# A gated hybrid encoder block on one core: a new order of its work groups, planned with other durations

## The chip, the cores and the metric

The kernel runs on one core of a Trainium2 chip. The metric is device time in microseconds (us) of one execution. Engines are named as in the profile: PE multiplies matrices (PEld loads its weights), DVE and POOL do elementwise work, ACT does activations and copies, SP issues nearly all the DMAs.

## The reference, cut to what matters

One layer over x (1024 rows, width 1024), in float32:

```
h = rmsnorm(x);  q, k, v, z_a, u_b, v_b, z_b, g_a, g_b = split(h @ w_in)
y_a = stick_breaking_attention(q, k, v) * silu(z_a)       # 8 heads of 64
y_b = spatial_gating(gelu(u_b), gelu(v_b)) * silu(z_b)    # 8 groups of 64, chunks of 128 rows
merged = sigmoid(g_a) * (y_a @ w_up_a) + sigmoid(g_b) * (y_b @ w_up_b)
out = rmsnorm(x + merged @ w_out)
```

In stick-breaking attention the weight of key s for query t is sigmoid(z[t,s]) times the product of sigmoid(-z) over the keys between s and t, so every row of scores needs a running product (a scan) over its keys. Spatial gating normalises gelu(v_b) per group, mixes it along 128 rows with a masked weight, adds a bias and multiplies by gelu(u_b).

## The kernel before, in words

**Numbers.** Every product is made of three float32r products (high·high, high·low, low·high). `hi_lo` (L214) makes the parts: ACT casts the high part, DVE (or POOL) subtracts to get the low part.

**Projections.** `project` (L528) makes one pair of 128-wide column tiles of h @ w_in for all 1024 rows by seven block products of 12 matmuls (84 matmuls of 512 columns), with sums and differences of weight blocks on POOL and DVE before them and sums of results after them. It uses the PSUM tiles X, Y, Z, four raw weight tiles `a` (7 slots) loaded by SP, split weights `b` (8 slots) and `f2`. There are 20 such work groups, each with a `use` of its four results:

- `make_kq` (4): split and store keys and queries to DRAM for one pair of heads.
- `make_za` (2): SiLU of attention's gate path. `make_gates` (8): sigmoid of the merge gates, ACT and a store only.
- `make_u`, `make_zb`, `make_vb` (2 halves of each): the spatial gate. `make_vb` is the long one: a GELU, transposes, reductions, scalings, a mixing product and transposes back, through the tiles `r`, `ak`, `e`, `tr`, `o`, `z`.

**Attention.** `head(p, h)` (L820) loads keys, queries and values (7 loads into 4 `k` tiles) and goes over two chunks of 512 queries. `attn_row` (L650) makes scores (PE, tile `z`), two sigmoids (ACT, tiles `ak`, `r`), the scan (DVE: `scan`, L198, on diagonal blocks; `scan_mult`, L191, on the others) and the product of the two (DVE on diagonal blocks, POOL on the others). `attn_step` (L674) transposes the weights (tile `tr`), splits them (`e`) and multiplies with the values (`o`). Heads share `r`, `ak`, `e`, `tr`, `o`, `z` with `make_vb`; `project` uses none of these.

**After the heads.** `up_b`, `up_a` (products of y_b, y_a with the up weights), then the output product and the last norm.

**What sets the order.** Nothing is issued as it is written. Each operation becomes a `Task` with an engine and a cost (L104 to L231). `Plan.issue` (L234) then plays the program against these costs: an engine that is free takes the ready task of the lowest priority number, a result reaches another engine `LAT` later, a tile is given out in the order in which the code first named the tiles of its tag. The order so found, engine by engine and for SP's DMA queue, is written into the program. On the chip each engine runs its own list in that order and waits where an operand is late; costs change the lists, never an operation.

For PE the priority number is the place in the code: what was written first goes first whenever it is ready, and later groups fill in. For the others it is that place plus an offset: -9000 for `project`'s own steps, -6000 for the `use` of a group called by `ahead` (L813), 0 otherwise. L827 to L854 name the groups in the order kq0 u0 zb0 vb0 za0 h0 u1 zb1 vb1 h1 kq1 g0 g1 h2 kq2 g2 h3 za1 g3 h4 kq3 g4 h5 g5 h6 g6 h7 g7 (h for heads, g for merge gates); those from u1 on that aren't heads go through `ahead`.

Of the kernel before, what the change touches and what calls it, by code (L numbers as in the profile page):

```python
# [10 lines left out]
F32 = mybir.dt.float32  # L11
# [9 lines left out]
EPS = 1e-6  # L21
GELU_C = 0.044715
GELU_S = 1.5957691216057308
LAT = 0.7
SCAN = 2.0


# [56 lines left out]


class Task:
    __slots__ = ("eng", "cost", "fn", "bufs", "deps", "users", "idx", "prio", "tail", "waiting", "ready", "end")


class Plan:  # L90
# [13 lines left out]
    def add(self, eng, cost, fn, out, ins, tail=0.0):  # L104
        t = Task()
        t.eng, t.cost, t.fn, t.tail = eng, cost, fn, tail
        t.idx = len(self.tasks)
        t.prio = t.idx + (self.offset if eng != "PE" else 0)
        t.deps, t.users, t.bufs = set(), [], []
        for v, write in [(v, True) for v in out] + [(v, False) for v in ins]:  # L110
            b = v.buf
            for box, w, other in b.touched:
                if (w or write) and other is not t and all(a < d and c < e for (a, e), (c, d) in zip(box, v.box)):
                    t.deps.add(other)
            b.touched.append((v.box, write, t))
            if b.order is None:
                b.order = self.tag_count.get(b.tag, 0)
                self.tag_count[b.tag] = b.order + 1
            if b not in t.bufs:
                t.bufs.append(b)  # L120
                b.left += 1
        for o in t.deps:
            o.users.append(t)
        self.tasks.append(t)


    def mm(self, out, lhsT, rhs, start, stop, **kw):
        self.add("PE", max(0.109, rhs.n * 0.000417 + 0.0135),
                 lambda: self.nc.tensor.matmul(out.ap(), lhsT=lhsT.ap(), rhs=rhs.ap(), start=start, stop=stop, **kw),  # L129
                 [out], [lhsT, rhs])  # L130

# [30 lines left out]

    def tt(self, out, in0, in1, op, eng="DVE"):
        e = self.nc.vector if eng == "DVE" else self.nc.gpsimd
        near = in0.buf.psum or in1.buf.psum
        cost = out.n * (0.001042 if near else 0.00135) + 0.15 if eng == "DVE" else out.n * 0.00252 + 0.24
        self.add(eng, cost, lambda: e.tensor_tensor(out=out.ap(), in0=in0.ap(), in1=in1.ap(), op=op),  # L167
                 [out], [in0, in1])

# [17 lines left out]
                 [out], [in_])  # L187

    def scan_mult(self, out, in_, init=None):
        self.add("DVE", in_.n * 0.00255 + 0.14,  # L190
                 lambda: self.nc.vector.tensor_tensor_scan(out.ap(), in_.ap(), in_.ap(),  # L191
                                                           1.0 if init is None else init.ap(), op0=ALU.mult,
                                                           op1=ALU.bypass),
                 [out], [in_] + ([] if init is None else [init]))

    def scan(self, out, in_, floor, init):
        self.add("DVE", in_.n * 0.00255 + 0.14,
                 lambda: self.nc.vector.tensor_tensor_scan(out.ap(), in_.ap(), floor.ap(), init, op0=ALU.mult,  # L198
                                                           op1=ALU.max), [out], [in_, floor])

# [31 lines left out]


    def issue(self):  # L234
        now, seq = 0.0, 0
        events = []
        ready = {}
        busy = {}
        turn = {}
        free = dict(self.slots)  # L240
        order = []
        for t in self.tasks:
            t.waiting, t.ready = len(t.deps), 0.0
            busy.setdefault(t.eng, 0.0)
            ready.setdefault(t.eng, [])
            if not t.deps:
                heapq.heappush(ready[t.eng], (t.prio, t.idx, t))

        def can_start(t):
            need = {}  # L250
            for b in t.bufs:
                if not b.held:
                    need.setdefault(b.tag, []).append(b.order)
            for tag, orders in need.items():
                nxt = turn.get(tag, 0)
                if free[tag] < len(orders) or sorted(orders) != list(range(nxt, nxt + len(orders))):
                    return False
            return True

        done = 0  # L260
        while done < len(self.tasks):
            started = False
            for eng, heap in ready.items():
                if busy[eng] > now + 1e-9:
                    continue
                skipped = []
                pick = None
                while heap:
                    item = heapq.heappop(heap)
                    if can_start(item[2]):  # L270
                        pick = item[2]
                        break
                    skipped.append(item)
                for item in skipped:
                    heapq.heappush(heap, item)
                if pick is None:
                    continue
                for b in pick.bufs:
                    if not b.held:
                        b.held = True  # L280
                        free[b.tag] -= 1
                        turn[b.tag] = turn.get(b.tag, 0) + 1
                order.append(pick)
                pick.end = now + pick.cost
                busy[eng] = pick.end
                seq += 1
                heapq.heappush(events, (pick.end, seq, 0, pick))
                done += 1
                started = True
            if started:  # L290
                continue
            if not events:
                stuck = [(t.idx, t.eng, [(b.tag, b.order, b.held, turn.get(b.tag, 0), free[b.tag]) for b in t.bufs])
                         for h in ready.values() for _, _, t in sorted(h)[:4]]
                raise RuntimeError(f"no operation can start: {stuck[:12]}")
            now = events[0][0]
            while events and events[0][0] <= now + 1e-9:
                _, _, kind, t = heapq.heappop(events)
                if kind == 1:
                    heapq.heappush(ready[t.eng], (t.prio, t.idx, t))  # L300
                elif kind == 2:
                    free[t] += 1
                elif kind == 0:
                    for u in t.users:
                        lag = t.tail if t.eng == "DMA" else 0.0 if u.eng == t.eng else LAT
                        u.ready = max(u.ready, now + lag)
                        u.waiting -= 1
                        if u.waiting == 0:
                            seq += 1
                            heapq.heappush(events, (max(u.ready, now), seq, 1, u))  # L310
                    for b in t.bufs:
                        b.left -= 1
                        if b.left == 0 and b.tag in free:
                            seq += 1
                            heapq.heappush(events, (now + t.tail + LAT, seq, 2, b.tag))
        self.length = max(t.end for t in self.tasks)
        for t in order:
            ins = t.fn()
            if t.eng != "DMA":
                self.tc.keep_in_program_order(ins)  # L320
# [9 lines left out]
def hybrid_block(  # L330
# [270 lines left out]
    def make_kq(p):  # L601
        def use(j, half, v, in_psum):
            hi, lo = buf("f2", dt=F32R), buf("f2", dt=F32R)
            pl.hi_lo(hi.all, lo.all, v, near(in_psum))
            pl.store(kq_hi[p][j, :, half_of(half)], hi.all)
            pl.store(kq_lo[p][j, :, half_of(half)], lo.all)
        project(KQ + p, use)

    za = [buf("d", (P, S)) for _ in range(4)]
# [203 lines left out]
    def ahead(fn, *args):  # L813
        pl.offset = -6000
        fn(*args)
        pl.offset = 0
# [7 lines left out]
                sums_of[p, ch] = buf("os")  # L824
            attn_step(*parts, p, h, ch, sums_of[p, ch])

    make_kq(0)  # L827
    make_u(0)
    make_zb(0)
    make_vb(0)  # L830
    make_za(0)
    head(0, 0)
    ahead(make_u, 1)
    ahead(make_zb, 1)
    ahead(make_vb, 1)
    head(0, 1)
    ahead(make_kq, 1)
    ahead(make_gates, 0)
    ahead(make_gates, 1)
    head(1, 0)  # L840
    ahead(make_kq, 2)
    ahead(make_gates, 2)
    head(1, 1)
    ahead(make_za, 1)
    ahead(make_gates, 3)
    head(2, 0)
    ahead(make_kq, 3)
    ahead(make_gates, 4)
    head(2, 1)
    ahead(make_gates, 5)  # L850
    head(3, 0)
    ahead(make_gates, 6)
    head(3, 1)
    ahead(make_gates, 7)  # L854


    ys = {}
# [192 lines left out]
```

## Time and profile before

| | us |
|---|---|
| median of 3 runs (lowest, highest) | 766.57 (766.36, 766.86) |
| the profiled execution, its own time | 766.53 |
| span of the trace in it | 764.7 |

The span runs from the first to the last instruction, 1.8 us less than the execution's time. The stretches of the program in this trace, by the tiles that PE writes: loads, norm and values to 70 us; groups kq0 to za0 and u1 from 70 to 198; head 0 with zb1 and vb1 from 198 to 250; kq1 and g0 until head 1 begins at 306; seven heads with the other ten groups and `up_b` until 632; then `up_a`, the output product and the last norm. A busy time counts a matmul from its start to its modelled end, and matmuls overlap, so short gaps between them don't show.

### The profile page before, as it was taken

How to read it: one execution, taken by the hardware profiler on the slowest of the kernel's cores; microseconds unless marked ns; L12 is line 12 of the kernel's file. 1: busy time of each engine (PE TensorE's matmuls, PEld its weight loads, DVE VectorE, ACT ScalarE, POOL GpSimd, SP SyncE). 2: the span in 40 equal slices, each digit the busy share in tenths (PEclk: the TensorE clock that was granted, in tenths of full speed). 3: DMA queues.
4: the chain of work that ended last, by engine and by line, in shares of the span. 5: the costliest groups of instructions: out<-in, count | busy, mean ns of one | idle time of the engine just before them, and what ended most of it. 6: DMA issues, size and time to landing. Idle time of an engine off the chain costs nothing.

```text
span 764.7 us, 10791 instructions
## 1 busy us (share of the span) xinstructions
PE 735.0 (96%) x3524; PEld 606.4 (79%) x3524; DVE 575.0 (75%) x788; ACT 433.5 (57%) x920; POOL 308.8 (40%) x298
## 2 busy tenths in 40 slices
PE   4989999999889999999999999999999999999996
PEld 3877788888777888887888888878888887888885
DVE  4868754688899787898999988897998878841122
ACT  6636474756756755666757676676867433411122
POOL 1500637497666576274345538234140300013110
PEclk9999999999999999999999999999999999999999
DMA  9412494424344375454543656354597677760022
GB/s 338 176 64 96 144 255 159 146 96 138 113 127 127 103 212 185 141 166 137 153 124 114 191 165 180 108 137 127 173 311 255 213 237 231 252 228 1 29 82 111
DMA packets 69177, 121.31 MB, mean 159 GB/s; under 512 B 7296, under 2 KB 17024, under 8 KB 69120
## 3 DMA queue, kind: packets, MB, share of 16 engines
q1 hardware_dynamic: 67968, 118.52, 49.3%
q10 hardware_dynamic: 1152, 2.10, 0.7%
q8 instruction: 28, 0.46, 0.3%
q14 instruction: 29, 0.24, 0.1%
HBM read 81.27 MB, written 39.32 MB: 158 GB/s over the span
## 4 chain that ended last, share of the span: by engine, by line
PE 83%; DVE 9%; issue 3%; DMA 2%; ACT 2%; POOL 1%; SPq 0%; POOLq 0%; DVEq 0%; ACTq 0%
PE Y L129 22%; PE X L129 21%; PE Z L129 18%; PE z L129 9%; PE o L129 8%; PE tr L133 5%; DVE b L167 2%; DVE ak L198 1%; DVE ak L191 1%; DMA k<-in_x_dram 1%; DVE e L167 1%; DMA k<-d 1%; DVE T L167 1%; DVE f L167 1%; DVE r L167 1%
## 5 line engine op out<-in xcount | busy, mean ns | idle before, releaser
L129 PE MATMUL Y<-T,b 128*128 128x512 f32 x672 | 180.0, 398 | 1.6 <-ACT b L157 1.3
L129 PE MATMUL X<-T,b 128*128 128x512 f32 x660 | 177.9, 398 | 0.0
L129 PE MATMUL Z<-T,b 128*128 128x512 f32 x540 | 145.2, 397 | 0.0
L129 PEld LDWEIGHTS Y<-T,b 128*128 128x128 f32 x672 | 122.3, 188 | 26.0 <-ACT b L157 1.7
L157 ACT CAST b<-a 128x512 fp32r<-128x512 f32 (+1 forms) x152 | 93.6, 617 | 81.9 <-PE Y L129 22.5
L129 PEld LDWEIGHTS X<-T,b 128*128 128x128 f32 x660 | 119.8, 188 | 22.8 <-POOL b L167 0.4
L167 DVE TENSOR_TENSOR b<-a,b 128x512 fp32r<-128x512 f32 (+1 forms) x112 | 99.4, 889 | 28.8 <-ACT b L157 20.0
L129 PEld LDWEIGHTS Z<-T,b 128*128 128x128 f32 x540 | 98.1, 188 | 18.3
L167 POOL TENSOR_TENSOR b<-a,b 128x512 fp32r<-128x512 f32 x40 | 60.7, 1516 | 119.8 <-ACT b L157 106.6
L198 DVE TENSOR_TENSOR_SCAN ak<-ak,c 128x128 f32<-128x128 f32 (+1 forms) x64 | 72.8, 1141 | 3.5 <-ACT ak L146 3.4
L167 POOL TENSOR_TENSOR a<-a,a 128x512 f32<-128x512 f32 x40 | 61.5, 1537 | 28.9 <-DVE b L167 15.3
L167 POOL TENSOR_TENSOR f<-f,f 128x512 f32<-128x512 f32 (+1 forms) x38 | 56.2, 1484 | 36.0 <-ACT f L146 14.7
L157 ACT CAST e<-tr 128x512 fp32r<-128x512 f32 (+1 forms) x96 | 45.7, 480 | 36.5 <-PE tr L133 33.3
L167 POOL TENSOR_TENSOR r<-r,ak 128x512 f32<-128x512 f32 x32 | 46.9, 1474 | 39.4 <-DVE ak L191 33.4
L133 PE MATMUL tr<-c,r 128*128 128x128 f32 x320 | 58.5, 273 | 2.6 <-DVE r L167 2.5
L129 PE MATMUL o<-e,k 128*128 128x512 f32 (+1 forms) x192 | 57.6, 343 | 3.3 <-DVE e L167 3.2
L146 ACT ACTIVATE ak<-z 128x128 f32<-128x128 f32 (+2 forms) x96 | 47.4, 494 | 20.4 <-PE z L129 18.1
L129 PE MATMUL z<-k,k 128*128 128x512 f32 (+2 forms) x216 | 56.8, 352 | 0.9 <-DMA k<-d 0.9
L167 DVE TENSOR_TENSOR e<-tr,e 128x512 fp32r<-128x512 f32 (+1 forms) x96 | 52.0, 545 | 7.3 <-ACT e L157 6.4
L146 ACT ACTIVATE r<-z 128x128 f32<-128x128 f32 (+2 forms) x96 | 46.9, 495 | 13.1 <-PE tr L133 12.5
L133 PEld LDWEIGHTS tr<-c,r 128*128 128x128 f32 x320 | 39.9, 140 | 13.6 <-DVE r L167 3.4
L191 DVE TENSOR_TENSOR_SCAN ak<-ak,c 128x512 f32<-128x512 f32 x32 | 50.5, 1588 | 0.2
(217 smaller groups left out, 1148.5 us busy)
## 6 DMA issues: line engine op xcount, KB each, us to landing
d<-f SPq DMA_DIRECT2D x112, 256.0 KB, 2.8
a<-in_w_pairs_dram SPq DMA_DIRECT2D x80, 256.0 KB, 2.8
f<-d SPq DMA_DIRECT2D x72, 256.0 KB, 3.2
k<-d SPq DMA_DIRECT2D x48, 256.0 KB, 4.8
k<-in_x_dram SPq DMA_DIRECT2D x8, 512.0 KB, 7.2
d<-b SPq DMA_DIRECT2D x16, 256.0 KB, 2.3
k<-d SPq DMA_DIRECT2D x8, 512.0 KB, 6.3
a<-in_w_up_dram SPq DMA_DIRECT2D x16, 256.0 KB, 4.3
```

The lines of the kernel that those rows point to most:

```text
L129: lambda: self.nc.tensor.matmul(out.ap(), lhsT=lhsT.ap(), rhs=rhs.ap(), start=start, stop=stop, **kw),
L133: self.add("PE", 0.109, lambda: self.nc.tensor.transpose(out=out.ap(), in_=in_.ap(), identity=ident.ap()), [out], [in_, ident])
L146: return self.nc.scalar.activation(out=out.ap(), in_=in_.ap(), func=func, scale=sc, **kw)
L157: lambda: self.nc.scalar.copy(out=out.ap(), in_=in_.ap()), [out], [in_])
L167: self.add(eng, cost, lambda: e.tensor_tensor(out=out.ap(), in0=in0.ap(), in1=in1.ap(), op=op), [out], [in0, in1])
L191: lambda: self.nc.vector.tensor_tensor_scan(out.ap(), in_.ap(), in_.ap(), 1.0 if init is None else init.ap(), op0=ALU.mult, op1=ALU.bypass),
L198: lambda: self.nc.vector.tensor_tensor_scan(out.ap(), in_.ap(), floor.ap(), init, op0=ALU.mult, op1=ALU.max), [out], [in_, floor])
```

## The change

Four things change in the planner's costs. LAT goes from 0.7 to 0.25 us. The costs of DVE's and POOL's two-operand operations and of scans are lowered. A matmul whose moving operand is float32 is charged twice. A task of DVE or POOL with more than one SBUF input of over 64 elements is marked `shared`, and marked tasks of the two engines are played one after the other (`port`). The groups are then named in the order of `ORDER`, where a word with a plus goes through `ahead`: both halves of u, zb and vb and za0 stand before head 0, kq1 between heads 1 and 2, six groups (g2 g0 kq2 g1 kq3 za1) between heads 2 and 3, g6 and g3 behind head 5, g4 and g5 behind head 6, g7 behind head 7. No operation is added or removed.

```diff
--- before.py
+++ after.py
@@ -21,7 +21,7 @@
 EPS = 1e-6
 GELU_C = 0.044715
 GELU_S = 1.5957691216057308
-LAT = 0.7
+LAT = 0.25
 SCAN = 2.0
 
 
@@ -84,7 +84,8 @@
 
 
 class Task:
-    __slots__ = ("eng", "cost", "fn", "bufs", "deps", "users", "idx", "prio", "tail", "waiting", "ready", "end")
+    __slots__ = ("eng", "cost", "fn", "bufs", "deps", "users", "idx", "prio", "tail", "waiting", "ready", "end",
+                 "shared")
 
 
 class Plan:
@@ -106,6 +107,7 @@
         t.eng, t.cost, t.fn, t.tail = eng, cost, fn, tail
         t.idx = len(self.tasks)
         t.prio = t.idx + (self.offset if eng != "PE" else 0)
+        t.shared = eng in ("DVE", "POOL") and len([v for v in ins if v.n > 64 and not v.buf.psum]) > 1
         t.deps, t.users, t.bufs = set(), [], []
         for v, write in [(v, True) for v in out] + [(v, False) for v in ins]:
             b = v.buf
@@ -125,7 +127,7 @@
 
 
     def mm(self, out, lhsT, rhs, start, stop, **kw):
-        self.add("PE", max(0.109, rhs.n * 0.000417 + 0.0135),
+        self.add("PE", max(0.109, rhs.n * 0.000417 + 0.0135) * (2 if rhs.buf.dt == F32 else 1),
                  lambda: self.nc.tensor.matmul(out.ap(), lhsT=lhsT.ap(), rhs=rhs.ap(), start=start, stop=stop, **kw),
                  [out], [lhsT, rhs])
 
@@ -162,8 +164,7 @@
 
     def tt(self, out, in0, in1, op, eng="DVE"):
         e = self.nc.vector if eng == "DVE" else self.nc.gpsimd
-        near = in0.buf.psum or in1.buf.psum
-        cost = out.n * (0.001042 if near else 0.00135) + 0.15 if eng == "DVE" else out.n * 0.00252 + 0.24
+        cost = out.n * 0.001042 + 0.14 if eng == "DVE" else out.n * 0.0024 + 0.06
         self.add(eng, cost, lambda: e.tensor_tensor(out=out.ap(), in0=in0.ap(), in1=in1.ap(), op=op),
                  [out], [in0, in1])
 
@@ -187,14 +188,14 @@
                  [out], [in_])
 
     def scan_mult(self, out, in_, init=None):
-        self.add("DVE", in_.n * 0.00255 + 0.14,
+        self.add("DVE", in_.n * 0.0021 + 0.15,
                  lambda: self.nc.vector.tensor_tensor_scan(out.ap(), in_.ap(), in_.ap(),
                                                            1.0 if init is None else init.ap(), op0=ALU.mult,
                                                            op1=ALU.bypass),
                  [out], [in_] + ([] if init is None else [init]))
 
     def scan(self, out, in_, floor, init):
-        self.add("DVE", in_.n * 0.00255 + 0.14,
+        self.add("DVE", in_.n * 0.0021 + 0.15,
                  lambda: self.nc.vector.tensor_tensor_scan(out.ap(), in_.ap(), floor.ap(), init, op0=ALU.mult,
                                                            op1=ALU.max), [out], [in_, floor])
 
@@ -232,7 +233,7 @@
 
 
     def issue(self):
-        now, seq = 0.0, 0
+        now, seq, port = 0.0, 0, 0.0
         events = []
         ready = {}
         busy = {}
@@ -282,6 +283,9 @@
                         turn[b.tag] = turn.get(b.tag, 0) + 1
                 order.append(pick)
                 pick.end = now + pick.cost
+                if pick.shared:
+
+                    pick.end = port = max(now, port) + pick.cost
                 busy[eng] = pick.end
                 seq += 1
                 heapq.heappush(events, (pick.end, seq, 0, pick))
@@ -824,34 +828,16 @@
                 sums_of[p, ch] = buf("os")
             attn_step(*parts, p, h, ch, sums_of[p, ch])
 
-    make_kq(0)
-    make_u(0)
-    make_zb(0)
-    make_vb(0)
-    make_za(0)
-    head(0, 0)
-    ahead(make_u, 1)
-    ahead(make_zb, 1)
-    ahead(make_vb, 1)
-    head(0, 1)
-    ahead(make_kq, 1)
-    ahead(make_gates, 0)
-    ahead(make_gates, 1)
-    head(1, 0)
-    ahead(make_kq, 2)
-    ahead(make_gates, 2)
-    head(1, 1)
-    ahead(make_za, 1)
-    ahead(make_gates, 3)
-    head(2, 0)
-    ahead(make_kq, 3)
-    ahead(make_gates, 4)
-    head(2, 1)
-    ahead(make_gates, 5)
-    head(3, 0)
-    ahead(make_gates, 6)
-    head(3, 1)
-    ahead(make_gates, 7)
+    ORDER = ("+kq0 u0 zb0 vb0 +za0 +u1 zb1 +vb1 h0 h1 kq1 h2 g2 +g0 +kq2 +g1 "
+             "+kq3 +za1 h3 h4 h5 g6 g3 h6 g4 g5 h7 +g7")
+    groups_of = {"kq": make_kq, "u": make_u, "zb": make_zb, "vb": make_vb, "za": make_za, "g": make_gates}
+    for word in ORDER.split():
+        name = word.strip("+0123456789")
+        n = int(word[-1])
+        if name == "h":
+            head(n // 2, n % 2)
+        else:
+            (ahead if word[0] == "+" else lambda fn, k: fn(k))(groups_of[name], n)
 
 
     ys = {}
```

## Rows read from the trace of the kernel before

**Rows 1.** The page, busy time, share of the span and instructions of each engine.
```profile
PE 735.0 (96%) x3524; PEld 606.4 (79%) x3524; DVE 575.0 (75%) x788; ACT 433.5 (57%) x920; POOL 308.8 (40%) x298
```

**Rows 2.** Busy time (instructions) by stage; stretch, its length, engines, clock, DMA share, GB/s.
```profile
core 0: us, PE busy (x) PEld busy (x) DVE busy (x) ACT busy (x) POOL busy (x), PEclk, DMA share, GB/s
0.00:20.00 20.00, 8.83 (x32) 7.00 (x33) 9.92 (x19) 12.48 (x22) 3.07 (x12) 1.00 0.94 342
20.00:70.00 50.00, 46.78 (x226) 38.03 (x224) 37.53 (x72) 26.46 (x66) 9.94 (x12) 1.00 0.29 106
70.00:198.00 128.00, 127.62 (x585) 105.10 (x586) 88.45 (x115) 79.31 (x138) 77.57 (x59) 1.00 0.51 152
198.00:250.00 52.00, 47.09 (x227) 37.65 (x226) 49.63 (x57) 33.23 (x75) 34.40 (x26) 1.00 0.41 125
250.00:306.00 56.00, 55.53 (x279) 46.24 (x278) 44.21 (x59) 34.09 (x62) 38.14 (x30) 1.00 0.53 167
306.00:632.00 326.00, 324.17 (x1609) 268.51 (x1609) 288.50 (x378) 213.47 (x490) 128.76 (x136) 1.00 0.56 172
632.00:660.00 28.00, 26.65 (x118) 21.73 (x117) 23.46 (x38) 12.99 (x23) 0.47 (x1) 1.00 0.79 253
660.00:764.70 104.70, 98.32 (x456) 82.10 (x455) 33.28 (x58) 21.51 (x49) 16.46 (x24) 0.99 0.29 101
```

**Rows 3.** Waits of PE in 198:250; us in total, times, longest.
```profile
PE tr L133 <- DVE r L167: 2.5, 2, 1.5
PE o L129 <- DVE e L167: 2.4, 3, 1.5
```

**Rows 4.** Timeline around 205 us; start, us, engine, line; [idle before <-releaser].
```profile
203.08 1.52 DVE L198 TENSOR_TENSOR_SCAN ak<-ak,c 128x128 f32<-128x128 f32 x1
...
204.28 1.39 POOL L167 TENSOR_TENSOR b<-a,b 128x512 fp32r<-128x512 f32 x1
204.73 1.08 DVE L167 TENSOR_TENSOR r<-r,ak 128x128 f32<-128x128 f32 x1
...
205.74 1.78 DVE L198 TENSOR_TENSOR_SCAN ak<-ak,c 128x256 f32<-128x256 f32 x1
...
205.87 0.33 PE L133 MATMUL tr<-c,r 128*128 128x128 f32 x1 [0.96 <-DVE r L167]
```

**Rows 5.** Whole run by line and form; xcount | busy us, mean ns | idle before.
```profile
L167 DVE TENSOR_TENSOR b<-a,b 128x512 fp32r<-128x512 f32 x108 | 95.7, 887 | 26.3 <-ACT b L157 17.5 <-PE Z L129 3.7 <-POOL b L167 3.2
...
L167 POOL TENSOR_TENSOR b<-a,b 128x512 fp32r<-128x512 f32 x40 | 60.7, 1516 | 119.8 <-ACT b L157 106.6 <-PE Y L129 5.1 <-PE z L129 3.5
...
L191 DVE TENSOR_TENSOR_SCAN ak<-ak,c 128x512 f32<-128x512 f32 x32 | 50.5, 1588 | 0.2
...
L198 DVE TENSOR_TENSOR_SCAN ak<-ak,c 128x512 f32<-128x512 f32 x16 | 25.0, 1560 | 2.9 <-ACT ak L146 2.9
...
L167 DVE TENSOR_TENSOR r<-r,s 128x512 f32<-128x512 f32 x8 | 11.8, 1478 | 0.3 <-POOL s L167 0.2
...
L167 POOL TENSOR_TENSOR T<-T,b 128x512 f32<-128x512 f32 x8 | 10.3, 1291 | 0.6
```

**Rows 6.** The same view, DVE in 580:600, where POOL stands idle.
```profile
L198 DVE TENSOR_TENSOR_SCAN ak<-ak,c 128x512 f32<-128x512 f32 x2 | 2.4, 1216 | 0.0
...
L167 DVE TENSOR_TENSOR b<-a,b 128x512 fp32r<-128x512 f32 x3 | 2.0, 683 | 0.0
```

**Rows 7.** Timeline around 603 us: a scan of an off-diagonal row beside POOL.
```profile
602.81 1.28 DVE L191 TENSOR_TENSOR_SCAN ak<-ak,c 128x512 f32<-128x512 f32 x1
602.86 2.33 POOL L167 TENSOR_TENSOR os<-os,f 128x512 f32<-128x512 f32 x1 [18.02 <-DVE os L167]
```

**Rows 8.** Timeline of PE: the last attention product, and the last fill behind it.
```profile
627.11 0.39 PE L129 MATMUL o<-e,k 128*128 128x512 f32 x1
...
644.56 2.88 PE L129 MATMUL X<-T,T 128*128 128x512 f32 x12
```

**Rows 9.** Waits of PE in 250:660.
```profile
PE z L129 <- DMA k<-d: 0.9, 2, 0.7
```

## The prediction, made before the changed kernel was run

> **What bounds the kernel now.** I read the page's busy times first: PE is busy 735.0 of 764.7 us [rows 1], so 29.7 us is all that a reordering could give back in the open. The table by stage says where that lies [rows 2]: 11.2 us in the first 20 us, where the DMA share is 0.94 and the first loads are awaited; 3.2 between 20 and 70; 0.4 between 70 and 198; 4.9 between 198 and 250; 0.5 until 306; 1.8 until 632; 1.4 until 660; 6.4 at the end, behind the last matmuls. The order of the groups touches neither the loads nor the end. The one stretch inside that stands out is 198 to 250: PE loses 9% of it and DVE is busy 49.6 of 52 us. There head 0 runs beside zb1 and vb1, the two groups that use DVE and POOL most.
>
> Busy time hides part of the loss, since a matmul's record overlaps the next. So I count instructions. In 306 to 632, where heads also run beside groups, PE starts 1609 in 326 us, 4.94 per us; in 198 to 250 it starts 227, which at that rate take 46.0 us [rows 2]. The stage therefore loses about **6.0 us**. PE's waits there name DVE, once for `r` and once for `e` [rows 3]. The timeline shows the pattern: POOL subtracts weights from 204.28 to 205.67, DVE's 128-wide product, begun at 204.73, ends only at 205.81, and PE's transpose starts 0.06 us behind it after 0.96 us of idleness [rows 4]. Nothing was missing but this one result, and PE, which follows its list, could not pass to the next group's matmuls.
>
> **Why the plan was wrong there.** The old costs give that 128-wide product 0.323 us (0.00135 a column plus 0.15); it took 1.08. The two scans around it, of 128 and 256 columns, were planned at 0.466 and 0.793 and took 1.52 and 1.78 [rows 4]. Where POOL stands idle, a 512-wide DVE product takes 0.683 and a 512-wide scan 1.216 [rows 6]; over the whole run they average 0.887 and 1.56 [rows 5]. The old cost of the first, 0.841, lies between free and mean; that of the scan, 1.446, too. So an operation is either free or blocked by POOL's whole instruction, and the old plan charged a middle value.
>
> **The change, part by part.**
>
> *Costs.* New: DVE product 0.674 at 512 columns, scan 1.225, POOL product 1.289. The free rows say 0.683, 1.216 and 1.291 [rows 5, 6], so all three now fit undisturbed operations. LAT 0.25 against 0.06 seen behind DVE [rows 4] is still on the safe side, but 0.45 us of slack is gone from every hand-over. Doubling matmuls with a float32 moving operand changes nothing: every `rhs` in the program is a float32r tile. Costs by themselves run on no engine; they alter the lists.
>
> *The port.* Serialising marked operations is what rows 4 show, and it lets the planner set PE's matmuls behind a blocked product instead of ahead of it. But the mark counts distinct views of over 64 elements. `scan_mult` passes one view twice and isn't marked, nor is vb's scaling, whose factor has 8 elements. The trace disagrees on both. A `scan_mult` of 1.28 us from 602.81 makes a POOL product begun at 602.86 last 2.33, over 1 us more than the free 1.291 [rows 5, 7]; scans of this kind average 1.588 and vb's scaling 1.478, more than twice the 0.683 of a free product of its width [rows 5, 6]. Unplanned: 32 × (1.588 - 1.225) = 11.6 us and 8 × (1.478 - 0.674) = 6.4 us of DVE, 18.0 in all. Cover: DVE has 37.5 us of idleness in 306 to 632 [rows 2]. If the cover were gone, all 18.0 would stand on PE's path; if it holds, nothing would. The old plan missed 0.14 us on each such scan too, and PE lost 1.8 us in that stage, so I take **+1.0**.
>
> The Trainium skill, "SBUF — State Buffer", section "SBUF: two separate sides", says that a DVE operation with two SBUF inputs and a GpSimd operation exclude each other for the whole instruction. By that, a scan that reads one tile twice belongs among the marked, against what this change does; the trace agrees (rows 7).
>
> *Groups.* u1, zb1 and vb1 go ahead of head 0. zb0, vb0, za0 and u1 run so today, between 70 and 198: 585 matmuls in 128 us, 0.4 us idle, DVE 69% busy [rows 2]. Their PE time is only moved. What vb1 brings to DVE moves out of the stage at 95% into one with room, and head 0 then runs beside kq1 and gates, as the other heads do. So the 6.0 goes: **-6.0** (between 0, if the waits only move, and the whole).
>
> Is there still enough to fill? Today seven heads, ten groups and most of `up_b` take 326 us with DVE at 88% [rows 2]. Afterwards head 0 and kq1 and g0 join them. Today these stand in 198 to 306; without zb1 and vb1 they need about a seventh of 326 us, 47. The mean load stays 88%. And the end gives room: the last attention product starts at 627.1, and PE has other matmuls until the group of 644.56 ends at 647.4 [rows 8], so a last head up to some 20 us later costs nothing directly.
>
> *Moved DMAs.* Head 0's seven loads are moved on SP's queue past the loads and stores of u1, zb1 and vb1, and every later group's four weight loads and its stores change place. Heads 0 and 1 become neighbours, so head 1's `k` tiles are reloaded close behind head 0, as at other joints. All those joints together made PE wait 0.9 us for `k` [rows 9]. At the new joint between vb1 and head 0 the shared tiles pass over in order, while PE has kq1. Bounds 0 and 3 (half of the loss of the stage that it replaces); I take **+0.5**, near the joints' row.
>
> *Elsewhere.* Idle between 20 and 70 and between 250 and 660 is 6.9 us [rows 2]. Lists made from truer costs may take some or add some: bounds -6.9 and +3 (again half of the loss at 198). I take **-1.0**, near zero, because half of that idleness lies between 20 and 70, where POOL is busy for 9.9 of 50 us and the port has little to say.
>
> **Sum.** The profiled execution took 766.53 us (span 764.7 and 1.8 around it), 0.04 under the median, so both are one number here. 766.53 - 6.0 + 1.0 + 0.5 - 1.0 = **761.0 us**.
>
> **Rivals.**
>
> *Slack gone, scans unplanned (slower).* Place: the off-diagonal rows of each head's second chunk, where `scan_mult` meets POOL, and vb's scaling. The plan thinks DVE done, sets PE's transposes and products close behind, and PE stands. Price: 18.0 us if all of it reaches PE, that is 766.5 - 6.0 + 18.0 = 778.5; at a half 769.5. It decides from a third of the 18.0, where it eats the gain. For it: 0.45 us less slack each time, and six groups have PE's priority between heads 2 and 3, which leaves later heads denser. Against it: DVE idle of 37.5 us and the spare 20 us at the end. Chance 0.27.
>
> *The waits only move (same).* vb1's four results meet kq1's weights, head 0 queues behind vb1 for `r`, `e`, `tr` and `o`, and what was lost at 198 is lost at 230. Price: the 6.0 comes back, 766 to 767. For it: the DVE work is the same. Against: vb0 passes the same joint with 0.4 us lost in 128 [rows 2]. That the lists hardly change, so that the change doesn't do what it says, would give the same time, but is unlikely, since every cost and the group order differ. Chance 0.14 together.
>
> *Truer plan everywhere (faster still).* The waits between 20 and 70 and after 250 go too: 766.5 - 6.0 - 6.9 = 753.6. For it: the new costs fit the free rows closely. Against: the early waits lie where POOL does little, so the port does not explain them. Chance 0.11.
>
> **Numbers.** The forecast has 0.48, the faster rival 0.11, the same 0.14, the slower one 0.27. 0.2% is 1.5 us, about what a measurement of this kernel tells from no change. The forecast's own range (757.5 to 764.5) lies below that line, so faster is 0.59, same 0.14, slower 0.27. The range for 8 in 10 starts at 754, just above the faster rival's full price, and reaches to 774, the slow rival at three quarters of its price.
>
> **What would show it.** In the changed profile: PE idle in the stretch that holds head 0 under 2 us in 50, DVE there under 92%; the stretch from 70 to the end of vb1 as dense as today's 70 to 198, with the 168 matmuls of zb1 and vb1 in it before the first score; PE's waits on `r` and `e` short. Scans of L191 still near 1.6 us. Wrong if PE's waits on DVE add up to over 10 us in the heads' stage (the slow rival), if the last attention product starts after 647, or if the early 20 to 70 us change by more than 3 us.

## The result and the profile after

The change is slower: 772.62 us (771.77 to 775.14, 4 runs) against 766.70, ratio 1.0083 with an interval of 1.0059 to 1.0108. The forecast was 761.0. The profiled execution took 775.14 us (span 773.4), the slowest of the four; it stands 8.6 us over the one of before.

Busy times of the page, then the table by stage over the same stretches as [rows 2], with clock, DMA share and GB/s in the last columns:

```profile
PE 739.1 (96%) x3524; PEld 609.9 (79%) x3524; DVE 559.9 (72%) x788; ACT 433.8 (56%) x920; POOL 300.7 (39%) x298
```
```profile
0.00:20.00 20.00, 9.73 (x42) 7.61 (x43) 10.60 (x20) 12.94 (x24) 3.20 (x12) 1.00 0.89 326
20.00:70.00 50.00, 46.60 (x215) 37.60 (x213) 37.93 (x71) 28.56 (x66) 9.19 (x12) 0.97 0.32 112
70.00:198.00 128.00, 124.30 (x564) 102.18 (x565) 88.69 (x111) 72.53 (x127) 74.37 (x54) 1.00 0.48 148
198.00:250.00 52.00, 52.00 (x245) 43.22 (x244) 32.76 (x46) 32.83 (x59) 38.11 (x27) 1.00 0.44 142
250.00:306.00 56.00, 55.28 (x278) 45.79 (x277) 47.62 (x66) 34.16 (x72) 30.80 (x31) 1.00 0.50 160
306.00:632.00 326.00, 316.10 (x1561) 260.87 (x1560) 271.51 (x363) 211.32 (x492) 124.31 (x136) 0.98 0.55 163
```

198 to 250 is dense now, as forecast. The loss is elsewhere: 306 to 632 starts 1561 matmuls instead of 1609 [rows 2], although DVE has more room (271.5 busy, 288.5 before), and two stretches show a granted clock under 1. PE's waits from 20 to 660 us (total, times, longest) name a new releaser, and the timeline of PE shows its two large cases:

```profile
PE z L131 <- DMA k<-d: 8.6, 6, 3.7
PE Y L131 <- ACT b L159: 1.6, 1, 1.6
PE o L131 <- ACT e L159: 1.6, 2, 1.2
PE tr L135 <- POOL r L168: 1.5, 2, 1.0
PE Y L131 <- DVE b L168: 1.2, 1, 1.2
PE X L131 <- DVE e L168: 1.0, 1, 1.0
```
```profile
355.68 1.17 PE L131 MATMUL Z<-T,b 128*128 128x512 f32 x4
359.33 0.30 PE L131 MATMUL z<-k,k 128*128 128x128 f32 x1 [2.48 <-DMA k<-d]
...
555.72 0.45 PE L131 MATMUL z<-k,k 128*128 128x128 f32 x1 [3.73 <-DMA k<-d]
```

The first scores of a head wait for its key tiles: 8.6 us where [rows 9] had 0.9. Behind both waits the clock falls. By stretch (columns as above):

```profile
360.00:364.00 4.00, 4.00 (x13) 3.22 (x12) 2.87 (x5) 1.90 (x4) 0.00 (x0) 0.57 1.04 245
364.00:400.00 36.00, 36.00 (x179) 29.57 (x178) 26.41 (x35) 21.60 (x47) 20.11 (x21) 1.00 0.40 133
...
555.00:562.00 7.00, 6.28 (x20) 5.44 (x21) 1.86 (x3) 1.78 (x6) 1.70 (x3) 0.51 0.93 261
562.00:580.00 18.00, 18.00 (x95) 14.87 (x94) 14.90 (x23) 10.07 (x24) 2.96 (x9) 1.00 0.87 277
```

0.51 and 0.57 mean that nearly all of the stretch ran at 1.2 of 2.4 GHz. At the rate of 562 to 580 (5.3 matmuls per us) the 6.28 us in which PE is busy there (the first 0.7 still belong to the wait) would have started 33 instead of 20: 2.5 us lost. 360 to 364 loses 7 of 20, another 1.4. A third fall, behind waits of 0.5 and 1.0 us at 40 to 43 us, is the 0.97 of the second stage; in 4.53 busy us between 42 and 47 PE starts 15 where the 4.6 per us behind it give 21, some 1.3 us.

So, in the profiled execution: -6.0 at 198 to 250; +7.7 of waits for keys; +5.2 of clock; +3.3 of PE idleness in 70 to 198 (3.7 against 0.4). That is +10.2; the other stages give back 1.6, the first 20 us (0.9) and 632 to 660 (1.4) above all. These are shares of one trace, and the counts behind the clock's part are good to some tenths.

Why the keys are late shows in SP's timeline and in the landing times of the `k<-d` loads from 230 to 600 us, after and (second line) before:

```profile
353.73 2.36 SPq L224 DMA_DIRECT2D k<-d  x4
...
357.62 0.45 SPq L224 DMA_DIRECT2D k<-d  x1
```
```profile
DMA to landing us min/median/max: 3.4/4.7/8.4
DMA to landing us min/median/max: 3.4/4.7/8.5
```

There are 6 `k` tiles and a head takes 4, so two of its tiles come free only when the head before has made its last scores, and their loads go out in a burst just ahead of the first scores. The plan lets a 256 KB load land 0.75 + 2.0 us after its turn on the DMA line; over all these loads (those of the values are of 512 KB) the median is 4.7 and the worst 8.4. Before, they took as long, and PE waited 0.9 us for them.

### The profile page after: what moved, and what is told of

The parts are those of the page before. It is cut to its first block, busy times and chain, and to the rows that moved or that the text cites. A ratio compares the mean times of both kernels' runs of the same rounds, so it can differ in the third digit from the quotient of the medians.

```text
span 773.4 us, 10783 instructions
## 1 busy us (share of the span) xinstructions
PE 739.1 (96%) x3524; PEld 609.9 (79%) x3524; DVE 559.9 (72%) x788; ACT 433.8 (56%) x920; POOL 300.7 (39%) x298
## 4 chain that ended last, share of the span: by engine, by line
PE 80%; DMA 7%; issue 4%; DVE 4%; POOL 3%; ACT 1%; SPq 1%; POOLq 0%; DVEq 0%; ACTq 0%
PE Y L131 20%; PE X L131 20%; PE Z L131 17%; PE z L131 9%; PE o L131 9%; PE tr L135 5%; DMA k<-d 4%; DMA k<-in_x_dram 1%; DVE T L168 1%; POOL a L168 1%; SPq L224 1%; POOL f L168 1%; DMA a<-d 1%; DMA a<-in_w_pairs_dram 1%; DVE b L168 1%
## 5 line engine op out<-in xcount | busy, mean ns | idle before, releaser
L131 PE MATMUL Z<-T,b 128*128 128x512 f32 x540 | 147.6, 398 | 0.0
L168 DVE TENSOR_TENSOR b<-a,b 128x512 fp32r<-128x512 f32 (+1 forms) x112 | 94.8, 847 | 50.3 <-ACT b L159 46.4
L168 POOL TENSOR_TENSOR b<-a,b 128x512 fp32r<-128x512 f32 x40 | 58.7, 1469 | 95.6 <-ACT b L159 89.7
L168 POOL TENSOR_TENSOR f<-f,f 128x512 f32<-128x512 f32 (+1 forms) x38 | 58.3, 1538 | 49.4 <-ACT f L148 23.7
L168 POOL TENSOR_TENSOR a<-a,a 128x512 f32<-128x512 f32 x40 | 59.1, 1478 | 30.3 <-DVE b L168 13.5
L168 POOL TENSOR_TENSOR r<-r,ak 128x512 f32<-128x512 f32 x32 | 44.5, 1396 | 64.7 <-DVE ak L192 48.8
L131 PE MATMUL z<-k,k 128*128 128x512 f32 (+2 forms) x216 | 59.9, 358 | 9.4 <-DMA k<-d 8.6
L199 DVE TENSOR_TENSOR_SCAN ak<-ak,c 128x128 f32<-128x128 f32 (+1 forms) x64 | 63.6, 1001 | 0.2 <-ACT ak L148 0.2
L135 PE MATMUL tr<-c,r 128*128 128x128 f32 x320 | 60.9, 275 | 1.5 <-POOL r L168 1.5
L131 PEld LDWEIGHTS z<-k,k 128*128 128x128 f32 x216 | 40.1, 192 | 18.8 <-issue 5.5
```

What stands on the lines that cost most here:

```text
L135: self.add("PE", 0.109, lambda: self.nc.tensor.transpose(out=out.ap(), in_=in_.ap(), identity=ident.ap()), [out], [in_, ident])
```

## The experiments

All are timed against the kernel before on the same chip in 3 rounds; from chip to chip its median lies between 766.5 and 767.2. "LAT", "durations" and "order" are the parts of the change.

**The two halves apart, and two single numbers.** e1 keeps the new costs with the old calls; e2 keeps all old costs under the new `ORDER` (its diff against before is the change's last part alone); e3 and e4 alter the change by one number:

```diff
 # e1
-    ORDER = ("+kq0 u0 zb0 vb0 +za0 +u1 zb1 +vb1 h0 h1 kq1 h2 g2 +g0 +kq2 +g1 "
...
+    make_kq(0)
+    make_u(0)
...
 # e3
-LAT = 0.25
+LAT = 0.7
 # e4, in load()
-                 tail=2.0)
+                 tail=5.0 if out.buf.tag == "k" else 2.0)
```

> The new costs (LAT, durations, port) with the group order of before. Theory A (late key loads: the plan puts a head's first scores before its key tiles land, PE stands and its clock falls behind the wait): the old order has groups between most heads, so fewer waits, but the same short planned landing; 766 to 769, PE waits on k loads 2 to 5 us. Theory B (the new group order is at fault, the costs are good): 762 to 765. Theory C (slack gone: LAT 0.25 makes PE wait for ACT, DVE and POOL at every hand-over): 770 to 773 with the waits spread, k loads under 2 us.

Measured 786.28, ratio 1.0245 (1.0218 to 1.0273).

> The new group order with all costs of before. A: 0.45 us more is planned behind each freed tile and the slower planned engines leave PE filled, so waits on k loads fall from 8.6 to about 3 us: 764 to 767. B: 770 to 773, as slow as the change. C: 760 to 763, the order's own gain of some 6 us without the lost slack.

Measured 763.32, ratio 0.9962 (0.9947 to 0.9976).

> The change with LAT back at 0.7, all else new (durations, port, order). C: 760 to 765, nearly all of the loss was the slack. A: waits on k loads fall only by the part that 0.45 us covers, from 8.6 to about 5 us, 766 to 770. B: 770 to 773.

Measured 767.47, ratio 1.0007 (0.9996 to 1.0018).

> The change with one number altered: loads into the head tiles k are planned to land 5.0 us after their turn on the DMA line instead of 2.0. A: PE's waits on k loads fall from 8.6 to under 2 us, no stretch at half clock is left behind 300 us, and the time falls by these 7 and by the clock's some 4: 760 to 765. B and C: no more than 2 us better, 770 to 773.

Measured 767.61, ratio 1.0016 (0.9999 to 1.0033). PE's waits for keys fall to 0.5 us.

The order is good by itself and the costs are what loses; theory B falls. The table by stage of e2 shows PE dense from 70 to 306 and part of the gain lost among the heads:

```profile
198.00:250.00 52.00, 52.00 (x243) 43.16 (x244) 35.46 (x49) 31.79 (x58) 39.84 (x28) 1.00 0.42 134
250.00:306.00 56.00, 56.00 (x281) 46.87 (x280) 47.08 (x62) 35.30 (x76) 29.05 (x30) 1.00 0.51 168
306.00:632.00 326.00, 321.44 (x1609) 265.93 (x1608) 287.14 (x382) 213.22 (x492) 123.94 (x137) 1.00 0.57 171
```

e4 bears theory A out in part. With the keys planned later, the waits for them and the falls behind them are gone, some 12 us in the change's trace. Only 5.0 us come back, and 767.6 lies above the 760 to 765: PE's waits for ACT's `e` grow from 1.6 to 4.8 us, and behind the longest of them, 2.5 us, the clock falls for 3.4 us.

```profile
PE o L131 <- ACT e L159: 4.8, 4, 2.5
...
PE z L131 <- DMA k<-d: 0.5, 1, 0.5
```

e1 was worse than any theory said. Its waits for keys, 4.8 us, are those of theory A; but PE also waits 5.8 us for ACT, DVE and POOL between 242 and 264 us, in the crowded old stretch, with the clock at 0.77.

**Both numbers at once, the port, the scans, and the later keys with old costs.** e6 and e7 alter the change, e5 too; e8 alters e2.

```diff
 # e5: the edits of e3 and e4; e8: the edit of e4
-                 tail=2.0)
+                 tail=5.0 if out.buf.tag == "k" else 2.0)
 # e6
-                if pick.shared:
+                if False:
 # e7, behind scan_mult's add and behind vb's scaling by wide(r)
+        self.tasks[-1].shared = True
```

> The change with LAT 0.7 and head-tile loads planned to land after 5.0 us, both at once. Theory A (what is lost are hand-overs planned too early, key loads first, and the clock that falls behind them): the 3.7 us wait for k and the 6.8 us at half clock of the run with LAT 0.7 go, 760 to 763, clock 0.999. If the two numbers mend the same waits, no better than each alone: 766 to 768.

Measured 771.04 (the median of three executions), ratio 1.0061 (1.0041 to 1.0082). The fourth, the profiled one, took 2620 us, so no trace of this list can be read. The two mends together are slower than either alone, which neither branch expected.

> The change without the serialised port (marked tasks are played like others), LAT 0.25 and new durations kept. If the port model does what the prediction gave it credit for, PE waits more for DVE and POOL results: 776 to 785. If it carries little, 770 to 774, as the change.

Measured 804.27, ratio 1.0475 (1.0437 to 1.0512): 31.7 us over the change. In the profiled execution (798.2) PE waits for DVE's `e` 17 times:

```profile
PE o L131 <- DVE e L168: 11.5, 17, 1.5
```

At these durations the port carries the plan, as far as one list of each kind can say.

> The change with the 32 scans of off-diagonal rows and vb's 8 scalings marked as well, as the trace says they should be. The prediction's slow rival (unplanned scans, 18 us of DVE, put PE's waits on DVE): the change's loss of 6 to 12 us goes, 760 to 766. Theory A: PE hardly waited for these, so nothing is won, 770 to 776, with waits on k loads still over 4 us.

Measured 790.19, ratio 1.0303 (1.0277 to 1.0328). Marking what the trace says is blocked gave a worse list, with 4.5 us in one wait for ACT:

```profile
PE z L131 <- DMA k<-d: 7.0, 4, 3.9
PE o L131 <- ACT e L159: 6.8, 4, 4.5
```

This alone doesn't clear the unplanned scans, since the list is another one. The change's own trace speaks against them: from 20 to 660 us PE's waits for DVE add up to 2.5 us there, those for POOL's `r` to 1.5.

> The new order, the costs of before, and head-tile loads planned to land after 5.0 us. A: the 1.9 us of waits on k loads in the run with the order alone go, 761 to 763. If later planned landings only push the heads back, 764 to 768.

Measured 762.29, ratio 0.9949 (0.9932 to 0.9965). No wait for keys is left; against e2 the intervals overlap.

**LAT by parts.** e9 alters e2. e11 and e12 split LAT in the change:

```diff
 # e9
-LAT = 0.7
+LAT = 0.25
 # e11 (e12 the other way round: 0.7 for engines, LAT elsewhere)
-  lag = ... else LAT
+  lag = ... else 0.7 if u.eng == "DMA" else LAT
-  heapq.heappush(events, (now + t.tail + LAT, seq, 2, b.tag))
+  heapq.heappush(events, (now + t.tail + 0.7, seq, 2, b.tag))
```

> The new group order, the durations of before without a port, and LAT 0.25: with the runs of the order alone (763.3), the change with LAT 0.7 (767.5) and the change itself (772.6) this fills the table of LAT against durations. If LAT is at fault by itself (hand-overs planned too early, whatever the durations): 767 to 771, with waits on k loads of 4 us or more. If the middle durations of before cover what LAT leaves out, 762 to 765; then only both new sets together lose.

Measured 781.07, ratio 1.0181 (1.0164 to 1.0198). LAT is at fault by itself, and by more than forecast: 17.8 us with the old durations (e9 against e2), 5.1 with the new ones and the port (the change against e3). Waits for keys are 6.5 us.

> The change with 0.7 us for the release of tiles and for results that a DMA waits for, 0.25 us for results that an engine waits for. Theory A (late key loads): this is the part of LAT that stands ahead of the loads, 765 to 769, waits on k loads halved to 4 us. Theory C (thin slack between engines): no better than 771.

Measured 776.89, ratio 1.0130 (1.0115 to 1.0145). Waits for keys fell to 2.4 us, yet it is slower than the change: a run of waits in vb1's chain between 263 and 276 us, the longest of 3.3 us, leaves PE at half clock for most of 14 us.

```profile
265.00:279.00 14.00, 8.03 (x29) 6.22 (x27) 9.46 (x10) 6.10 (x14) 11.10 (x14) 0.51 0.55 189
```

> The opposite: 0.7 us for results that an engine waits for, 0.25 us for the release of tiles and for DMAs. C: 764 to 768. A: 770 to 773, waits on k loads still 7 us or more.

Measured 770.74, ratio 1.0038 (1.0015 to 1.0062); keys 5.2 us. Neither half of LAT decides: shortening one wait made a list with another. One list also differs from execution to execution: the ten of e12 run from 767.4 us, at a granted clock of 0.998, to 774.6 at 0.991.

**How far neighbours differ.** e15 is e9 with the edit of e4. e10 and the two of e16 alter LAT in the change, e14 and e18 in e2; e13 is e8 with an order picked from many by the length of its plan:

```diff
 # e10 (0.24 and 0.30 in the two of e16)
-LAT = 0.25
+LAT = 0.27
 # e14 (0.75 in e18)
-LAT = 0.7
+LAT = 0.68
 # e13
+    ORDER = ("kq0 u0 +zb0 u1 +vb0 za0 zb1 vb1 kq1 h0 kq2 h1 +g0 h2 "
+             "h3 za1 g1 h4 g2 +g4 g6 +kq3 h5 +g3 +g7 h6 +g5 h7")
```

> The new order, old durations, LAT 0.25 (781.1 in an earlier run) with head-tile loads planned to land after 5.0 us. If the key loads are what LAT 0.25 loses by (theory A), most of the 17.8 us between LAT 0.7 and 0.25 goes: 763 to 768. If the hand-overs between engines lose as much (theory C), 771 to 778, with waits on k loads under 1 us and PE's other waits behind 20 us still over 12 us in sum (15.9 at LAT 0.25 without the longer landing).

Measured 776.15, ratio 1.0138 (1.0101 to 1.0176); no wait for keys, 16.9 us of others. With old durations only 5 of the 17.8 us that LAT 0.25 costs are keys. Planning the keys later thus took the waits for them to 0.5 us or none in all three lists with a trace (e4, e8, e15), and the time fell by 5.0, 1.0 (within the intervals) and 4.9 us; in the fourth list (e5 against e3) it rose by 3.6.

> The change with LAT 0.27 instead of 0.25: a neighbour that should differ by nothing but the luck of the list. 770 to 775 if differences of 5 us between settings mean something; outside of 767 to 778 they don't.

Measured 765.84, ratio 0.9991 (0.9982 to 1.0000). By the expectation's own terms, differences of 5 us between settings then mean little, those of e3 and e4 included; what carries their reading is the traces. Keys still take six waits, but the longest is 1.1 us and no fall follows them:

```profile
PE z L131 <- DMA k<-d: 3.9, 6, 1.1
```

> The new order with the costs of before and LAT 0.68 instead of 0.7: the same test of luck beside the run with the order alone (763.3). 761 to 766 if that gain is the order's own; 766 or more if it hung on one lucky list.

Measured 764.27, ratio 0.9970 (0.9959 to 0.9981).

> Costs of before, head-tile loads planned to land after 5.0 us, and a group order found by trying many against this plan (spatial gate ahead of attention, one or two groups between most heads). If these costs make a plan that the chip keeps, 757 to 761; if the choice only found a plan that flatters itself, 763 to 768.

Measured 762.08, ratio 0.9945 (0.9930 to 0.9960): faster than both kernels, not to be told from e8.

> The change with LAT 0.24. Its neighbour at 0.27 took 765.8, the change at 0.25 772.6. If the change's list is one bad draw among near ones (two key loads that come 2.5 and 3.7 us late, and a clock that falls behind both): 764 to 770. If 0.27 was the lucky one: 771 to 776.

Measured 770.93, ratio 1.0061 (1.0044 to 1.0078). One wait for keys of 2.3 us had no fall behind it, so a single wait of that length doesn't decide.

> The change with LAT 0.30: the other side of the same question. One bad draw: 764 to 770; 0.27 lucky: 771 to 776. [...]

Measured 780.43, ratio 1.0184 (1.0157 to 1.0212), worse than either side of the question. Keys take 6.6 us in six waits, none over 1.7. The longest wait, 3.1 us, is for ACT; it lies in the one fall before the end of the run, of 10.2 us, with others for ACT and keys around it.

> The new order with the costs of before and LAT 0.75: with 0.68 (764.3) and 0.70 (763.3) the spread of the old costs. 762 to 766 if the order's gain holds across lists; over 767 if it doesn't.

Measured 764.09, ratio 0.9972 (0.9956 to 0.9988).

The new order under both sets of durations, by LAT:

| LAT | 0.24 | 0.25 | 0.27 | 0.30 | 0.68 | 0.70 | 0.75 |
|---|---|---|---|---|---|---|---|
| new durations and port | 770.9 | 772.6 | 765.8 | 780.4 | | 767.5 | |
| durations of before | | 781.1 | | | 764.3 | 763.3 | 764.1 |

With the old costs three neighbours lie within 1.0 us. With the new durations and a small LAT four lie within 14.6. All of the four are slower than the order alone; which of them is bad, and through which wait, changes with a few hundredths of LAT.

## Why the prediction was wrong

**The gain of 6.0** came in its stage: 198 to 250 is full, and with the old costs the order is faster. But the whole got 3.2 us of it (766.5 to 763.3 in e2), half: among the heads PE stands 4.6 us, with 1.8 before. Part of the reading behind the term was off. [rows 3] counts two waits for `r` and three for `e`, not one each. And some 30 of DVE's 49.6 us in that stage are head 0's own scans, products and splits, while vb1's scalings run from 264 to 295 us, in the next one: the stage is dense now because head 0 has left it.

**The step that failed is "Moved DMAs", +0.5 with bounds of 0 and 3.** It priced the heads' joints by the 0.9 us that PE waited for keys before. That row held for the old list alone: the waits for keys are 1.9 us with the new order (e2), 4.0 with the new durations besides (e3), 6.5 with LAT 0.25 besides (e9) and 8.6 with both. The joint that the prediction looked at, between heads 0 and 1, cost 0.7 us; the long waits stand before heads 2 and 6. The row to read was another: how long such a load takes to land (4.7 us) against what the plan grants it (2.75). The term measured 7.7 us, and the clock behind the two long waits, which stood in no term, 3.9 more. Why the old list hid landings of the same length is not shown.

**"LAT 0.25 is still on the safe side"** rested on 0.06 us behind one DVE result, and that was the wrong test. LAT also stood in for what the plan prices too low, and e9 and e15 show that these are not the landings alone: with keys planned later PE still waits 16.9 us for ACT, DVE and POOL. In the change, PE's longest waits for `e` from ACT (1.2 us, behind a small load) and for `r` from POOL (1.0 us) lie in 70 to 198, which the prediction took to be as dense as before.

**Elsewhere, -1.0**, went the other way: 3.3 us in 70 to 198 and 1.3 in the early fall of the clock, less the 1.6 that the other stages give back (the remainder of the sum), are +3.0. With -6.0, 7.7 and 3.9 this makes the 8.6 of the profiled execution.

**Scans, +1.0.** Still unplanned (L192 averages 1.544), and PE's waits for DVE from 20 to 660 add up to 2.5 us, 8.2 before. The slow rival, which the prediction gave 0.27, had the right sign, and 772.6 lies between its half and its full price (769.5 and 778.5), but by another way: that is luck. Only its clause on lost slack held.

**The port.** That PE would be set behind blocked products was right, and worth 31.7 us at these durations (e6 against the change, one list each).

**The signs of being wrong.** One of the three came: the last attention product starts behind 647.

```profile
649.56 0.39 PE L131 MATMUL o<-e,k 128*128 128x512 f32 x1
```

It cost nothing directly, as the prediction had allowed: behind 660 us PE stands 6.4 us, as before. The other two, on waits for DVE and on the first 70 us, didn't come, and no sign looked at waits for DMAs.

**What stays open:** whether the new durations lose by themselves at LAT 0.7. 767.5 against 763.3 is one list each, and e3's trace has one wait of 3.7 us for keys and 6.8 us at half clock behind it, together more than the difference. Nor is it known what the loss would be on an average over lists: all five with the new order, durations and port (LAT from 0.24 to 0.7) are slower than e2, by 2.5 to 17.1 us, and not all through the same waits.

## What to carry to other kernels

A static order is as good as its least certain duration: before a planner's slack is cut, compare each kind of planned duration with its spread in the trace, DMA landings first, and keep the slack where the spread is; for the keys this paid 5 us in two lists of four, one was unclear and one lost. Test a plan with two or three neighbouring settings; if they differ by more than the gain, the gain is a draw. Change the order of work and the costs of the plan in separate steps: here the one was worth 3 us and the other cost more.

## What the runs showed of the hardware that was not expected

One late operand can cost more than its wait. Behind waits of 2.48 and 3.73 us PE ran at 1.2 GHz for 3.4 and 6.8 us and lost 1.4 and 2.5 us more. The Trainium skill, "TensorE: Matmul & The Clock Gate", section "Part 1: The HAM clock gate (the "warmup" mystery)", names these two levels and an idle engine as the reason for the lower; the trace agrees. The kernel before never left 2.4 GHz between 20 and 660 us [rows 2].

The length of the wait alone doesn't tell whether the clock falls. No fall came behind waits for keys of 2.28 us (LAT 0.24) and 2.87 us (e6):

```profile
469.25 0.47 PE L131 MATMUL z<-k,k 128*128 128x128 f32 x2 [2.87 <-DMA k<-d]
...
469.00:479.00 10.00, 9.75 (x56) 8.46 (x56) 6.25 (x12) 4.88 (x12) 3.13 (x4) 1.00 0.88 267
```

And the change's fall at 43 us stands behind waits of 0.5 and 1.0 us, where the kernel before waits 1.4 and 0.7 us and keeps 2.4 GHz.
